# Rounding and splitting streamed weights two row blocks per operation in a hybrid attention and recurrence layer

## The chip, the cores and the metric

The kernel runs on one core of a Trainium2 chip. Its time is the device time of one execution in microseconds (us); the lower, the better. A core has five engines with an instruction stream each: TensorE (PE, matmuls; its weight loads are shown as PEld), VectorE (DVE), ScalarE (ACT), GpSimd (POOL) and SyncE (SP), which here issues most of the DMA transfers. Engines wait for each other by semaphores and otherwise run on their own.

## The reference: what is computed

One layer with 512 tokens of width 2048, in float32. A root-mean-square norm of x is projected by one matrix `w_in` into queries, keys and values, an attention gate, a recurrence input and a recurrence gate. Attention (8 heads, 2 key and value heads, rotary positions) and a gated linear recurrence in both directions run in parallel; each result is normed, multiplied by a gate, and both go through one output matrix `w_out`, with x added.

```
h = rms_norm(x, norm_w)
proj = jnp.einsum('bsd,de->bse', h, w_in)
q, k, v, g_attn, xr, g_lru = jnp.split(proj, SPLITS, axis=-1)
attn_out = attention_group(q, k, v, q_norm_w, k_norm_w)
lru_out = lru_group(xr, conv_w, conv_b, lru_wa, lru_ba, lru_wx, lru_bx, lru_lambda)
mixed = jnp.concatenate([rms_norm(attn_out, attn_norm_w) * jax.nn.silu(g_attn),
                         rms_norm(lru_out, lru_norm_w) * jax.nn.silu(g_lru)], axis=-1)
return x + jnp.einsum('bse,ed->bsd', mixed, w_out)
```

## The kernel before

Every large product is done in three passes of a rounded type (`mm3`, L150 to L154). A float32 operand is split into a high part, rounded to float32r, and a low part, the difference, also rounded. The product is high times high, plus high times low, plus low times high: three matmuls of 128x128 by 128x512 in place of one. Both operands are split. The activations are split once and stay; the weights are streamed and split as they come.

A weight chunk is two row blocks: 256 rows of the matrix by 512 columns. It lands by one DMA in a raw tile `wr` of shape [128, 2, 512] (three such buffers). `wsplit` takes one of the two row blocks: ScalarE copies it to the high tile `wh` (L224, the rounding), then VectorE subtracts high from raw into the low tile `wl` (L226). So a chunk costs two roundings and two subtractions of 512 columns, and fills two high and two low tiles. Each kind of tile has four buffers in the pool `xw`; for a part of the kernel a second pool, `wx`, with four more of each is open, and the halves of a chunk take turns between the two.

The stages, in order of time:

- Two projections of the recurrence input (`proj_feat`, up to about 111 us), with the loading and transposing of x in the first, and the recurrence itself beside the second. Up to the third chunk the order of ScalarE and VectorE is written out by hand; after that the compiler orders them by priority and its estimate of the time. For the very first chunk, the two halves are split at different moments, since its rows land one after the other: the first half is rounded by VectorE in two pieces, the second by ScalarE.
- Keys and values, then queries (`tok_block`, to about 255 us). `wx` is opened during the queries and closed after them.
- The gate stage (`gates`, about 255 to 441 us), beside attention. Two kinds of unit alternate in an order written out as a string: `u`, a chunk of the recurrence gate (`gl_units`: 12 matmuls for two row blocks of 512 columns, some of them with a second operand `dh`, `dl` that is split too, L1199 and L1200), and `G` or `H`, a chunk of a quarter of the attention gate (`ga_units`: two row blocks of 256 columns, split in one operation each, L1227 and L1228, into one narrow tile of each kind). Both kinds draw on the same four buffers in `xw`.
- The rest of the attention gate (`proj_feat`, to about 485 us), while the operands of the output product are split into seven combinations (`seven`, L783 and L784, at 768 and 1024 columns).
- The output product (`outputs`, to the end), with a splitting of its own (`operand`, L802 and L803), its order written out by hand.

TensorE's instructions are issued in the program's order throughout. SyncE issues the weight loads in the order that the compiler gives them; the loads and splits carry a raised priority (`AHEAD = 600`). `paced` (L319) lets GpSimd copy one column of a low tile to hold back transfers of its own until that chunk is split.

Of the kernel before, what the change touches and what calls it, by code (L numbers as in the profile page):

```python
# [12 lines left out]
F32R = mybir.dt.float32r  # L13
# [4 lines left out]
P = 128  # L18
SEQ = 512
# [30 lines left out]
H = 256  # L50
# [12 lines left out]
def hybrid_kernel(  # L63
# [20 lines left out]
    nc = tc.nc  # L84
# [4 lines left out]
    pools, order = {}, {"left": [], "right": []}  # L89
# [25 lines left out]
    def nm(s):  # L115
        cnt[0] += 1
        return f"{s}_{cnt[0]}"
# [27 lines left out]
    def const(shape, name, dt=F32):  # L145
        return cp.tile(list(shape), dt, tag=name, name=name)

    def f(ap):
        return ap.bitcast(F32)
# [34 lines left out]
    def columns(dst, src):  # L184

        n = src.shape[0]
        pt = mm()
        nc.tensor.transpose(pt[:, :n], src, ident[:n, :n])
        with tc.high_priority():
            nc.vector.tensor_copy(dst, pt[:, :n])  # L190
# [22 lines left out]

    turn_of = [0]

    def wsplit(raw, k, rounded=nc.scalar.copy, parts=1):

        turn_of[0] += k
        pool = pools["wx" if "wx" in pools and turn_of[0] % 2 else "xw"]
        hi = pool.tile([P, SEQ], F32R, tag="wh", bufs=4, name=nm("wh"))  # L220
        lo = pool.tile([P, SEQ], F32R, tag="wl", bufs=4, name=nm("wl"))
        cols = [slice(n * SEQ // parts, (n + 1) * SEQ // parts) for n in range(parts)]
        for c in cols:
            rounded(hi[:, c], raw[:, k, c])  # L224
        for c in cols:
            nc.vector.tensor_sub(lo[:, c], raw[:, k, c], f(hi[:, c]))  # L226
        return hi, lo

    def wload(w, r0, c0):
        with tc.high_priority(AHEAD):  # L230
            (raw,) = wraw(w, r0, c0)
            return [wsplit(raw, k) for k in range(2)]


    xh, xl = [None] * KT, [None] * KT
# [824 lines left out]
    with tc.high_priority():  # L1060
        queues = nc.sync, nc.sync
        xs, ws = xload(0, queues), wraw_first(w_in, 0, C_XR, nc.sync)
        nc.scalar.dma_start(nw_st, norm_w.rearrange("(k p) -> k p", p=P))
        xc, raw = next(xs), next(ws)
        next(xs), next(ws)
        table = const([P, 1], "table")
        nc.scalar.activation(table, ones[:, :1], AF.Exp)
        columns(nw, nw_st)
        rest = list(xturn(xc, 0, 2))
        first = [wsplit(raw, 0, nc.vector.tensor_copy, 2)]  # L1070
        for r in rest:
            r()
        busy(WARM2)
# [3 lines left out]
    for step in proj_feat(C_XR, a1, first, given):  # L1077
        if step is None:
            with tc.high_priority():
                first.append(wsplit(raw, 1))  # L1080
                turned_x(xc, 1)
            xsquare(xc, 0)
            next(next(loads), None)
            given[1] = wload(w_in, 2 * P, C_XR)
            continue
        c, e = step
        if (e == 0 or e == 2) and c:
            next(next(loads, iter(())), None)
        if (e, c) == (2, 0) or (e == 1 and c) or (e, c) in ((3, 1), (3, 2)):
            next(next(turns, iter(())), None)  # L1090
        if (c, e) == (1, 2):
            given[2] = wload(w_in, 4 * P, C_XR)
            s2.close()
        if (c, e) == (2, 3):
            vec_load()
        if (c, e) == (5, 3):
            columns(vec, vec_st)
        if c == KT // 2 - 2 and e in (0, 1):
            with tc.high_priority():
                next(stats, None)  # L1100
            gate_maps.setdefault(0, []).extend(itertools.islice(maps, 2))
# [82 lines left out]
    def gl_units(banks):  # L1184

        nd = 0
        for name, left, right in PRODUCTS:
            for c in range(4):
                with tc.high_priority(AHEAD):
                    raw = pools["wr"].tile([P, 2, SEQ], F32, tag="wr", bufs=3, name=nm("wr"))  # L1190
                    nc.sync.dma_start(
                        raw, gsum[c][right] if isinstance(right, int) else two_gl(c, *right)
                    )
                    if isinstance(left, int):
                        draw = draws[nd % 2]
                        nd += 1
                        nc.sync.dma_start(draw, dsum[c][:, left])
                        dh, dl = d_tiles()
                        nc.scalar.copy(dh, draw)  # L1199
                        nc.vector.tensor_sub(dl, draw, f(dh))  # L1200
                    ws = [wsplit(raw, n) for n in range(2)]
                for n, (wh, wl) in enumerate(ws):
                    i = 2 * c + n
                    for s, bank in enumerate(banks):
                        if isinstance(left, int):
                            lh, ll = (t[:, n, s * P : (s + 1) * P] for t in (dh, dl))
                        else:
                            k, t = left
                            ts_ = slice(t * H + s * P, t * H + (s + 1) * P)
                            lh, ll = xh[2 * i + k][:, ts_], xl[2 * i + k][:, ts_]  # L1210
                        mm3(bank, lh, ll, wh, wl, i == 0, i == KT // 2 - 1)
                    if i == KT // 2 - 1:
                        product_done(name, banks)
                    yield name if i == KT // 2 - 1 else None

    def ga_units(part, res, banks):

        for c in range(KT // 2):
            with tc.high_priority(AHEAD):
                raw = pools["wr"].tile([P, 2, SEQ], F32, tag="wr", bufs=3, name=nm("wr"))  # L1220
                src = w_in[c * 2 * P : (c + 1) * 2 * P, C_GA + part * H : C_GA + (part + 1) * H]
                nc.sync.dma_start(raw[:, :, :H], src.rearrange("(k p) e -> p k e", p=P))
                wh, wl = (
                    pools["xw"].tile([P, SEQ], F32R, tag=t, bufs=4, name=nm(t)) for t in ("wh", "wl")
                )
                wh, wl = (t.rearrange("p (k e) -> p k e", k=2) for t in (wh, wl))
                nc.scalar.copy(wh, raw[:, :, :H])  # L1227
                nc.vector.tensor_sub(wl, raw[:, :, :H], f(wh))  # L1228
            for e, bank in enumerate(banks):
                es = slice(e * P, (e + 1) * P)  # L1230
                for k in range(2):
                    kk = 2 * c + k
                    mm3(
                        bank, wh[:, k, es], wl[:, k, es], xh[kk], xl[kk], kk == 0, kk == KT - 1
                    )
                if c == KT // 2 - 1 and e == 1:
                    res.extend(evac_bc(banks))
                yield None
# [165 lines left out]
```

## Time and profile before

| what | value |
|---|---|
| median of 3 runs | 642.55 us (642.46 to 642.91) |
| span of the profiled execution | 640.7 us |
| TensorE busy | 636.0 us, 99% |
| VectorE busy | 509.9 us, 80% |
| ScalarE busy | 382.2 us, 60% |
| GpSimd busy | 131.7 us, 21% |
| roundings of weight blocks at 512 columns (L224, ScalarE) | 151, together 90.1 us |
| subtractions (L226, VectorE) | 153, together 105.6 us |

The profile gives one execution of its own, 640.7 us from its first to its last instruction; the median of the runs is 1.85 us above that span. In the lines below, a row of the timeline gives the start in us from the beginning of the span, the duration in us, the engine, the line of the kernel, the operation, what it writes and reads, its shape, how many in a row, and in square brackets the idle time of the engine before it with what ended it. A row of the groups gives the busy time of the group in us, the mean of one instruction in ns, and the idle time before them. Tile names come without their buffer numbers, and a matmul's row names the moving operand first, then the stationary one.

### The profile page before, as it was taken

The page shows a single profiled execution, that of the slowest core. Times are in us where ns is not written, and L with a number is a line of the kernel's source. Part 1 is how long each engine was busy: PE and PEld are TensorE (multiplying, and loading weights), DVE is VectorE, ACT ScalarE, POOL GpSimd, SP SyncE. Part 2 cuts the span into 40 slices and gives each one's busy share as a digit, 9 for nine tenths or more (in the row PEclk, how much of TensorE's full clock was granted, in tenths as well). Part 3 has the DMA queues.
Part 4 walks back from the last instruction along what each step waited for, and adds up shares of the span by engine and source line. Part 5 has one row for each costly group of instructions (what it writes and reads, how often), then busy time and mean ns, then how long its engine had stood idle before and what let it go on. Part 6 is the DMA issues. An engine that isn't in the chain of part 4 may idle for free.

```text
span 640.7 us, 8950 instructions
## 1 busy us (share of the span) xinstructions
PE 636.0 (99%) x2962; PEld 528.3 (82%) x2962; DVE 509.9 (80%) x886; ACT 382.2 (60%) x725; POOL 131.7 (21%) x173
## 2 busy tenths in 40 slices
PE   9999999999999999999999999999999999999997
PEld 7888888888888888888888888888888888888886
DVE  5777679996698994977678877559938988698994
ACT  3543799489954624877666775946444754344441
POOL 0013403222150501412444353322000000110000
PEclk9999999999999999999999999999999999999999
DMA  8847976897757646445989997875565857585322
GB/s 295 293 140 202 242 203 154 247 252 182 186 158 196 203 135 196 137 141 162 239 241 280 252 253 225 196 209 149 131 196 204 295 175 248 185 281 208 122 93 99
DMA packets 68782, 128.19 MB, mean 200 GB/s; under 512 B 5504, under 2 KB 24320, under 8 KB 68480
## 3 DMA queue, kind: packets, MB, share of 16 engines
q1 hardware_dynamic: 55856, 90.25, 43.2%
q0 software_dynamic: 12704, 37.23, 25.3%
q8 instruction: 23, 0.38, 0.2%
q14 instruction: 23, 0.19, 0.1%
q10 hardware_dynamic: 176, 0.14, 0.1%
HBM read 119.21 MB, written 41.95 MB: 252 GB/s over the span
## 4 chain that ended last, share of the span: by engine, by line
PE 99%; DVE 0%; issue 0%
PE pj L152 19%; PE pj L153 19%; PE pj L154 19%; PE mm L1008 13%; PE pj L1008 11%; PE mm L152 3%; PE mm L154 3%; PE mm L153 3%; PE mm L655 2%; PE mm L256 1%; PE pj L332 1%; PE pj L349 1%; PE mm L591 1%; PE mm L1253 1%; PE mm L1047 0%; PE mm L741 0%
## 5 line engine op out<-in xcount | busy, mean ns | idle before, releaser
L224 ACT CAST wh<-wr 128x512 fp32r<-128x512 f32 x151 | 90.1, 618 | 70.6 <-PE pj L154 25.4
L226 DVE TENSOR_TENSOR wl<-wr,wh 128x512 fp32r<-128x512 f32 (+1 forms) x153 | 105.6, 713 | 30.9 <-ACT wh L224 29.6
L152 PE MATMUL pj<-x,wh 128*128 128x512 f32 x240 | 95.1, 396 | 0.0
L152 PE MATMUL pj<-wh,x 128*128 128x512 f32 x240 | 93.9, 391 | 0.0
L154 PE MATMUL pj<-x,wl 128*128 128x512 f32 x240 | 93.5, 390 | 0.0
L153 PE MATMUL pj<-x,wh 128*128 128x512 f32 x240 | 93.5, 390 | 0.0
L154 PE MATMUL pj<-wh,x 128*128 128x512 f32 x240 | 93.4, 389 | 0.0
L153 PE MATMUL pj<-wl,x 128*128 128x512 f32 x240 | 93.4, 389 | 0.0
L802 ACT CAST oh<-rw 128x512 fp32r<-128x512 f32 x94 | 56.3, 621 | 38.8 <-PE mm L1008 15.5
L803 DVE TENSOR_TENSOR ol<-rw,oh 128x512 fp32r<-128x512 f32 x94 | 61.8, 687 | 10.8 <-ACT oh L802 9.2
L154 PEld LDWEIGHTS pj<-x,wl 128*128 128x128 f32 x240 | 45.0, 188 | 9.7
L154 PEld LDWEIGHTS pj<-wh,x 128*128 128x128 f32 x240 | 45.0, 188 | 9.5
L152 PEld LDWEIGHTS pj<-wh,x 128*128 128x128 f32 x240 | 45.1, 188 | 9.3
L152 PEld LDWEIGHTS pj<-x,wh 128*128 128x128 f32 x240 | 45.1, 188 | 9.2
L153 PEld LDWEIGHTS pj<-wl,x 128*128 128x128 f32 x240 | 45.1, 188 | 9.1
L153 PEld LDWEIGHTS pj<-x,wh 128*128 128x128 f32 x240 | 45.1, 188 | 8.7
L1008 PE MATMUL mm<-oh,ml 128*128 128x512 f32 (+1 forms) x128 | 49.0, 382 | 0.0
L1008 PE MATMUL mm<-ol,mh 128*128 128x512 f32 (+1 forms) x128 | 48.9, 382 | 0.0
L1008 PE MATMUL mm<-oh,mh 128*128 128x512 f32 (+1 forms) x128 | 48.9, 382 | 0.0
L940 POOL DMA_DIRECT2D out_dram<-xt x12 | 6.6, 548 | 178.7 <-DVE xt L976 129.1
L1008 PE MATMUL pj<-oh,mh 128*128 128x512 f32 (+1 forms) x104 | 39.7, 382 | 0.0
L1008 PE MATMUL pj<-ol,mh 128*128 128x512 f32 (+1 forms) x104 | 39.7, 382 | 0.0
(243 smaller groups left out, 1341.4 us busy)
## 6 DMA issues: line engine op xcount, KB each, us to landing
wr<-in_w_in_dram SPq DMA_DIRECT2D x59, 512.0 KB, 4.4
rw<-in_w_out_dram SPq DMA_DIRECT2D x63, 256.0 KB, 3.6
gs<-in_w_in_dram POOLq DMA_DIRECT2D x24, 512.0 KB, 6.8
ts<-in_w_out_dram POOLq DMA_DIRECT2D x24, 512.0 KB, 7.3
wr<-gs SPq DMA_DIRECT2D x16, 512.0 KB, 5.3
rw<-ts SPq DMA_DIRECT2D x31, 256.0 KB, 4.7
wr<-in_w_in_dram SPq DMA_DIRECT2D x17, 256.0 KB, 4.3
gs<-gs POOLq DMA_DIRECT2D x8, 512.0 KB, 7.5
```

Of the source, the lines that this page charges most:

```text
L152: nc.tensor.matmul(acc, lh, rh, start=start, stop=False)
L153: nc.tensor.matmul(acc, lh, rl, start=False, stop=False)
L154: nc.tensor.matmul(acc, ll, rh, start=False, stop=stop)
L224: rounded(hi[:, c], raw[:, k, c])
L226: nc.vector.tensor_sub(lo[:, c], raw[:, k, c], f(hi[:, c]))
L256: nc.tensor.transpose(pt[:, t * P : (t + 1) * P], xc[:, h * n + t, ks], ident)
L332: nc.tensor.matmul(acc[e], w[:, e * P : (e + 1) * P], x_[k], start=k == 0 and j == 0, stop=False,)
L655: nc.tensor.transpose(pt[:, s * P : (s + 1) * P], p[:, s * P : (s + 1) * P], ident)
L802: nc.scalar.copy(hi, src)
L803: nc.vector.tensor_sub(lo, src, f(hi))
L940: (queue or nc.gpsimd).dma_start(of[t * P : (t + 1) * P, os_], xts[g][t][:, cs])
L1008: nc.tensor.matmul(bank[key][:, to], lh[:, a, ts_], rh[:, cols], start=i == 0 and j == 0, stop=i == 7 and j == 2,)
```

## The change

The two row blocks of a chunk are rounded by one ScalarE operation over [128, 2, 512] and subtracted by one VectorE operation of the same shape: 1024 columns in place of 512. The high and low tiles are [128, 2, 512], two buffers of each in place of four narrow ones, so their memory stays the same. `wpair` draws a pair of tiles, and the turn between `xw` and `wx` now goes by pairs. The very first chunk still splits its halves apart, into the two halves of one pair. A unit of the attention gate in the gate stage draws a whole wide pair too and uses 256 of each 512 columns. The matmuls, their order and the transfers are the same.

```diff
--- before.py
+++ after.py
@@ -213,23 +213,26 @@
 
     turn_of = [0]
 
-    def wsplit(raw, k, rounded=nc.scalar.copy, parts=1):
-
-        turn_of[0] += k
+    def wpair():
+
+        turn_of[0] += 1
         pool = pools["wx" if "wx" in pools and turn_of[0] % 2 else "xw"]
-        hi = pool.tile([P, SEQ], F32R, tag="wh", bufs=4, name=nm("wh"))
-        lo = pool.tile([P, SEQ], F32R, tag="wl", bufs=4, name=nm("wl"))
+        return [pool.tile([P, 2, SEQ], F32R, tag=t, bufs=2, name=nm(t)) for t in ("wh", "wl")]
+
+    def wsplit(raw, pair, ks=slice(0, 2), rounded=nc.scalar.copy, parts=1):
+
+        hi, lo = pair
         cols = [slice(n * SEQ // parts, (n + 1) * SEQ // parts) for n in range(parts)]
         for c in cols:
-            rounded(hi[:, c], raw[:, k, c])
+            rounded(hi[:, ks, c], raw[:, ks, c])
         for c in cols:
-            nc.vector.tensor_sub(lo[:, c], raw[:, k, c], f(hi[:, c]))
-        return hi, lo
+            nc.vector.tensor_sub(lo[:, ks, c], raw[:, ks, c], f(hi[:, ks, c]))
+        return [(hi[:, k], lo[:, k]) for k in range(ks.start, ks.stop)]
 
     def wload(w, r0, c0):
         with tc.high_priority(AHEAD):
             (raw,) = wraw(w, r0, c0)
-            return [wsplit(raw, k) for k in range(2)]
+            return wsplit(raw, wpair())
 
 
     xh, xl = [None] * KT, [None] * KT
@@ -1067,7 +1070,8 @@
         nc.scalar.activation(table, ones[:, :1], AF.Exp)
         columns(nw, nw_st)
         rest = list(xturn(xc, 0, 2))
-        first = [wsplit(raw, 0, nc.vector.tensor_copy, 2)]
+        pair = wpair()
+        first = wsplit(raw, pair, slice(0, 1), nc.vector.tensor_copy, 2)
         for r in rest:
             r()
         busy(WARM2)
@@ -1077,7 +1081,7 @@
     for step in proj_feat(C_XR, a1, first, given):
         if step is None:
             with tc.high_priority():
-                first.append(wsplit(raw, 1))
+                first.extend(wsplit(raw, pair, slice(1, 2)))
                 turned_x(xc, 1)
             xsquare(xc, 0)
             next(next(loads), None)
@@ -1198,7 +1202,7 @@
                         dh, dl = d_tiles()
                         nc.scalar.copy(dh, draw)
                         nc.vector.tensor_sub(dl, draw, f(dh))
-                    ws = [wsplit(raw, n) for n in range(2)]
+                    ws = wsplit(raw, wpair())
                 for n, (wh, wl) in enumerate(ws):
                     i = 2 * c + n
                     for s, bank in enumerate(banks):
@@ -1220,10 +1224,7 @@
                 raw = pools["wr"].tile([P, 2, SEQ], F32, tag="wr", bufs=3, name=nm("wr"))
                 src = w_in[c * 2 * P : (c + 1) * 2 * P, C_GA + part * H : C_GA + (part + 1) * H]
                 nc.sync.dma_start(raw[:, :, :H], src.rearrange("(k p) e -> p k e", p=P))
-                wh, wl = (
-                    pools["xw"].tile([P, SEQ], F32R, tag=t, bufs=4, name=nm(t)) for t in ("wh", "wl")
-                )
-                wh, wl = (t.rearrange("p (k e) -> p k e", k=2) for t in (wh, wl))
+                wh, wl = (t[:, :, :H] for t in wpair())
                 nc.scalar.copy(wh, raw[:, :, :H])
                 nc.vector.tensor_sub(wl, raw[:, :, :H], f(wh))
             for e, bank in enumerate(banks):
```

## The prediction

> **What bounds the kernel now.** I read the page's busy shares first, then its chain that ended last, then the waits of TensorE alone, then windows by stage, then single instructions at the places where the change could reach TensorE.
>
> ```profile
> PE 636.0 (99%) x2962; PEld 528.3 (82%) x2962; DVE 509.9 (80%) x886; ACT 382.2 (60%) x725; POOL 131.7 (21%) x173
> ...
> PE 99%; DVE 0%; issue 0%
> ```
>
> ```profile
> PE mm L1047 <- DVE ones L159: 1.0, 1, 1.0
> ```
>
> ```profile
> 0.00:20.00 20.00, 18.93 (x94) 15.05 (x95) 12.03 (x41) 8.24 (x14) 0.76 (x7) 1.00 0.80 264
> 20.00:57.00 37.00, 37.00 (x184) 30.81 (x182) 28.64 (x97) 14.58 (x26) 4.73 (x8) 1.00 0.67 214
> 255.00:441.00 186.00, 186.00 (x920) 155.47 (x919) 141.67 (x242) 135.79 (x291) 66.00 (x81) 1.00 0.76 205
> 485.00:641.00 156.00, 152.10 (x694) 126.57 (x692) 130.21 (x204) 71.03 (x119) 6.57 (x12) 1.00 0.57 196
> ```
>
> The chain is TensorE for 99% of the span. Its one listed wait is 1.0 us before its first matmul; the windows (columns: PE, PEld, DVE, ACT, POOL, then clock, DMA share, GB/s) show it busy without a gap from 20 us on, until the last stores, at the full clock (1.00). A busy row alone proves little, since matmul ends are modelled, so I went to the starts: the 128x512 matmuls quoted below follow each other every 0.227 us in every stage, although one is shown as 0.39 us long. So TensorE is fed without a hole. What ScalarE and VectorE save returns nothing to the span; what they deliver late is added to it in full, because behind any hole TensorE runs on at its one rate.
>
> **What one operation costs.** A pair (two row blocks) is now rounded on ScalarE (L224) and subtracted on VectorE (L226) in two operations each.
>
> ```profile
> L224 ACT CAST wh<-wr 128x512 fp32r<-128x512 f32 x151 | 90.1, 618 | 70.6 <-PE pj L154 25.4
> L226 DVE TENSOR_TENSOR wl<-wr,wh 128x512 fp32r<-128x512 f32 (+1 forms) x153 | 105.6, 713 | 30.9 <-ACT wh L224 29.6
> ```
>
> ```profile
> L784 DVE TENSOR_TENSOR ml<-t,mh 128x1024 fp32r<-128x1024 f32 x8 | 9.8, 1220 | 0.3 <-ACT mh L783 0.3
> L783 ACT CAST mh<-t 128x1024 fp32r<-128x1024 f32 x8 | 8.4, 1053 | 5.8 <-DVE t L774 5.8
> ```
>
> ```profile
> 17.47 1.14 ACT L224 CAST wh<-wr 128x512 fp32r<-128x512 f32 x2
> ...
> 17.04 1.41 DVE L259 SCALAR_TENSOR_TENSOR x<-mm,nw,x 128x512 fp32r<-128x512 f32 x2 [2.12 <-ACT x L258]
> ...
> 19.40 0.42 DVE L269 SCALAR_TENSOR_TENSOR b<-b 128x256 f32<-128x256 f32 x1
> ...
> 19.74 1.29 DVE L226 TENSOR_TENSOR wl<-wr,wh 128x512 fp32r<-128x512 f32 x2
> ```
>
> L783 and L784 do the same two operations at 1024 columns elsewhere: 1.05 and 1.22 us. By the means one would expect a pair to fall from 2 x 618 = 1.24 to 1.05 us, and from 2 x 0.71 = 1.43 to 1.22. But two in a row overlap: they take 1.14 and 1.29. Where they stand in a row, then, the real saving is 0.09 us per pair on ScalarE and 0.07 on VectorE. Over the kernel (151 roundings are 75 pairs and the second half of the first pair, which stays apart) L224 falls from 90.1 to 75 x 1.05 + 0.62 = 79 us busy and L226 from 105.6 to about 75 x 1.22 + 1.4 = 93, none of it on the path. The opposite cost is delivery: the first half's high part comes 1.05 - 0.62 = 0.43 us later, its low part 1.22 - 0.69 = 0.53 us later. Only places with less spare than that matter.
>
> **Place 1: the third chunk of the first projection (20 us).** Here ScalarE and VectorE still run in the written order, and VectorE comes to the subtraction late.
>
> ```profile
> 20.09 0.48 PE L152 MATMUL pj<-x,wh 128*128 128x512 f32 x1
> 20.48 0.19 PEld L154 LDWEIGHTS pj<-x,wl 128*128 128x128 f32 x1
> ```
>
> The low half is done at 19.74 + 0.69 = 20.43 and its weight load starts at 20.48: 0.05 us to spare. One wide subtraction ends at 19.74 + 1.22 = 20.96, so the load waits about 0.5 us. VectorE cannot come earlier: the squares of x (L269) stand ahead of it in the written order, behind L259, which waits for ScalarE at 17.04. Bounds: 0 (if the squares fell behind the subtraction, which the written order excludes) to 0.53. I take **+0.5**.
>
> **Place 2: the last chunk of the second projection (106 us).**
>
> ```profile
> 100.32 0.39 PE L152 MATMUL pj<-x,wh 128*128 128x512 f32 x1
> 105.11 1.29 DVE L226 TENSOR_TENSOR wl<-wr,wh 128x512 fp32r<-128x512 f32 x2
> 105.76 0.39 PE L152 MATMUL pj<-x,wh 128*128 128x512 f32 x1
> 105.99 0.19 PEld L154 LDWEIGHTS pj<-x,wl 128*128 128x128 f32 x1
> ```
>
> A wide subtraction ends at 105.11 + 1.22 = 106.33; the load is due at 105.99: 0.34 us late. TensorE's own 0.5 us of lateness from place 1 lends some of it back, if VectorE's work before is not itself held by TensorE, and the compiler may order VectorE otherwise. Bounds 0 and 0.34; I take **+0.2**, the middle.
>
> In the other chunks of these projections a tile comes free every 24 matmuls, 105.76 - 100.32 = 5.4 us, and rounding and subtracting want 1.05 + 1.22 = 2.27: nothing there. While the second weight pool is open there are four wide pairs instead of eight narrow ones: the same depth.
>
> **Place 3: the gate stage (255 to 441 us).** Units of 12 matmuls alternate between the two gates, and the tiles are one ring. Before, four narrow tiles; a gate unit of 256 columns (L1227, L1228) took one and a recurrence unit two, and the first half came free halfway through its unit. Now there are two wide ones, and either kind takes one, so unit n can be rounded only once unit n-2 is wholly done. The cover is one unit and what attention puts beside it. One of the narrowest:
>
> ```profile
> 335.46 0.39 PE L154 MATMUL pj<-wh,dl 128*128 128x512 f32 x1
> 335.69 0.39 PE L152 MATMUL pj<-wh,dh 128*128 128x512 f32 x1
> 339.20 0.48 PE L152 MATMUL pj<-wh,dh 128*128 128x512 f32 x1
> 339.52 0.40 PE L153 MATMUL pj<-wl,dh 128*128 128x512 f32 x1
> 337.04 0.78 ACT L646 ACTIVATE k<-mm,mx,q_r 128x512 f32<-128x512 f32 x1
> 337.72 0.19 ACT L646 ACTIVATION_READ_ACCUMULATOR k<-mm,mx,q_r 128x1 f32 x1
> 338.44 1.13 DVE L1228 TENSOR_TENSOR wl<-wr,wh 128x512 fp32r<-128x512 f32 x1 [0.28 <-ACT wh L1227]
> ```
>
> The tile is free at 335.69 and its low part is due at 339.52: 3.83 us for 2.27, 1.56 to spare. An exponential with its read (0.97) caught on ScalarE and a subtraction (0.68) on VectorE would use it up and 0.1 more; when VectorE runs stretched (1.13 for a 512-wide one) 0.5 more. I count five such windows (258, 280, 299, 336 and 354 us): 0 to 2.5 us; **+0.1**, since the loads carry the highest priority in that stage. At the stage's end the cover is smallest:
>
> ```profile
> 437.69 0.39 PE L154 MATMUL pj<-x,wl 128*128 128x512 f32 x1
> 440.64 0.39 PE L152 MATMUL pj<-x,wh 128*128 128x512 f32 x1
> 441.10 0.39 PE L154 MATMUL pj<-x,wl 128*128 128x512 f32 x1
> 437.31 1.21 DVE L784 TENSOR_TENSOR ml<-t,mh 128x1024 fp32r<-128x1024 f32 x1
> ```
>
> Free at about 437.92, low part due by 440.9: 3.0 for 2.27. A 1.05 us rounding and a 1.21 us subtraction of the output operands may stand in front: 0 to 1.5; I take **+0.1**.
>
> **Edits at nothing.** The loads on SyncE keep their order and their three buffers; a raw buffer comes free after its second subtraction, as before. GpSimd's marker (L319) waits for the end of the pair as before. The output stage (from 485 us) has its own rounding (L802) and is untouched.
>
> A rule against the change: the Trainium skill, Perfetto Trace Analysis, section Optimizing Scalar/DVE Operations, says grouping pays on a saturated engine, and that where the two are not saturated but hold up another, breaking operations up lets work finish sooner. By its second half the sum holds place 1 and 2 alone, 643.3; by its first half nothing is won with VectorE at 80%, which the trace bears out.
>
> **Sum.** 0.5 + 0.2 + 0.1 + 0.1 = +0.9 us on the profiled span of 640.7, so 641.6. The runs' median, 642.55, stands 1.85 above that span; I keep this: **643.5 us**. Worst of the bounds: 0.53 + 0.34 + 2.5 + 1.5 = 4.9, 647.4.
>
> **Rivals.**
> A, slower: in the gate stage ScalarE, in order, stands at a rounding whose tile is not free, and holds the exponentials behind it; their PSUM banks come late.
>
> ```profile
> 348.78 0.78 ACT L646 ACTIVATE k<-mm,mx,q_r 128x512 f32<-128x512 f32 x1
> 350.11 0.48 PE L152 MATMUL mm<-kt,b 128*128 128x512 f32 x1
> ```
>
> This score bank is read until 349.56 and I take it that the one written at 350.11 is the same: 0.55 us of spare. A hold of 1 us in each of eight heads costs 8 x 0.45 = 3.6 us: 647.1 with the rest. For it: half the depth. Against: the same wait exists already (25.4 us of L224's idle time) and costs nothing. It decides from holds over 0.55 us.
>
> B, slower: the two halves of the first pair now share a tile; were the whole tile waited for, its low part (first loaded at 7.37) would wait for the second half (8.23 + 0.69 = 8.92): +1.5, so 645.0.
>
> ```profile
> 7.37 0.77 PEld L332 LDWEIGHTS pj<-x,wl 128*128 128x128 f32 x4
> 8.23 0.69 DVE L226 TENSOR_TENSOR wl<-wr,wh 128x512 fp32r<-128x512 f32 x1 [0.96 <-ACT wh L224]
> 608.09 0.68 DVE L978 TENSOR_TENSOR xt<-xt,pj 128x512 f32<-128x512 f32 x1
> 608.58 0.54 POOL L940 DMA_DIRECT2D out_dram<-xt  x1 [44.87 <-DVE xt L976]
> ```
>
> Against: at 608 us one half of a tile is written while the store of its other half, ahead of it in the program, has not begun; parts are followed singly.
>
> C, faster: the saved 11 and 13 us bring TensorE work forward. All that could come forward is its first idle 1.07 us (20.00 - 18.93), 641.5, and that lies ahead of any weight.
>
> D, no change: place 1 is absorbed by a shift of VectorE: 642.6.
>
> **How the numbers follow.** Forecast 0.48, A or a large place 3 0.27, B 0.05, C 0.03, D 0.17. A difference under 0.2% (1.3 us) is about what a measurement of this kernel cannot tell from none. The forecast's +0.9 lies inside it, but a fifth of that case reaches over 643.84. Same: 0.17 + 0.38 = 0.55, slower 0.27 + 0.05 + 0.10 = 0.42, faster 0.03. The range runs from D less the scatter of the runs, 642.3, to 646.9, which leaves out C and the upper half of A. The likeliest case's own range is 642.8 to 644.3.
>
> **What would show it.** ScalarE about 371 us and VectorE about 497 busy in all (11 and 13 less); a wide rounding of 1.05 and a wide subtraction of 1.22; a hole of 0.5 us in TensorE's starts near 20.5 us and a smaller one near 106; 0.227 us elsewhere. Many holes between 260 and 441 us would show A. The prediction is wrong if the compiler's new order starves a stage that now has 2 us to spare, or if place 1 does not open.

## The result, and the profile after

The changed kernel took 648.94 us (median of four runs, 648.42 to 650.37), the kernel before 642.66 in the same series: a ratio of 1.0102, 95% interval 1.0088 to 1.0117. The forecast was 643.5 with a range up to 646.9. The profiled execution has a span of 646.3 us and took 648.42. Two executions of a later series, one of the kernel before (918 us at a mean granted clock of 0.66) and one of `one_pair` (1079 us at 0.56), are left out of every ratio below.

The page of the changed kernel: busy shares, the shares of the chain that ended last, and the groups of the rounding and the subtraction (its lines are numbered three higher than before).

```profile
PE 637.1 (99%) x2962; PEld 527.3 (82%) x2962; DVE 501.9 (78%) x811; ACT 373.9 (58%) x650; POOL 133.2 (21%) x173
...
PE 83%; DVE 7%; DMA 4%; ACT 4%; issue 2%; SPq 0%; DVEq 0%; ACTq 0%
...
L227 ACT CAST wh<-wr 128x1024 fp32r<-128x1024 f32 (+1 forms) x76 | 79.0, 1042 | 67.4 <-PE pj L153 22.4
L229 DVE TENSOR_TENSOR wl<-wr,wh 128x1024 fp32r<-128x1024 f32 (+2 forms) x78 | 93.2, 1196 | 31.3 <-ACT wh L227 28.9
```

The groups cost what was forecast, 79 and 93 us. VectorE and ScalarE are each 8 us less busy in all (13 and 11 were forecast; other operations took a little longer). TensorE's share still reads 99%, which tells nothing. The chain tells more: TensorE held 99% of it before and 83% now; VectorE, ScalarE and DMA have come into it. So do TensorE's waits (us in total, times, longest):

```profile
PE mm L152 <- ACT b L487: 2.5, 1, 2.5
PE pj L154 <- DVE wl L229: 1.3, 3, 0.8
PE mm L1050 <- DVE ones L159: 1.0, 1, 1.0
PE pj L152 <- ACT ev L555: 0.3, 1, 0.3
```

Before, only the third of these (as L1047) was there. Since TensorE's matmuls come in the same order in both, I subtracted the start of each matmul before from its start after; every jump of that difference is a hole. In this trace: 0.5 us at 20 us (place 1), **2.7 at 95 us**, 1.1 at 106 (place 2), 0.7 at 209 (queries), 0.35 from 350 to 358, 0.55 at 441 (end of the gate stage, at 446 here); the first loads gave some 0.5 back. At its end TensorE is 5.4 us late.

**The hole of 2.7 us** is in the second projection, where the recurrence's gate products (`mm<-k,k`) run between the weights. The timeline of the changed kernel, rows of five engines followed backward from the hole:

```profile
98.17 0.50 PE L152 MATMUL mm<-k,k 128*128 128x512 f32 x1 [2.49 <-ACT b L487]
...
92.07 0.69 ACT L487 ACTIVATE b<-mm,vec 128x512 f32<-128x512 f32 x1
95.97 0.62 ACT L460 CAST k<-k 128x512 fp32r<-128x512 f32 x1 [3.21 <-DMA k<-in_lru_wx_dram]
...
82.66 0.37 SPq L203 DMA_DIRECT2D wr<-in_w_in_dram  x1
83.08 0.46 SPq L538 DMA_DIRECT2D k<-in_k_norm_w_dram  x1
...
92.93 0.38 SPq L441 DMA_DIRECT2D k<-in_lru_wa_dram  x1
...
91.15 0.23 DVE L541 COPY k<-k 128x128 f32<-128x128 f32 x1 [3.62 <-DMA k<-in_k_norm_w_dram]
...
91.48 1.43 DVE L546 TENSOR_TENSOR rk<-rk,k 128x256 f32<-128x256 f32 x4
...
81.37 1.07 POOL L857 DMA_DIRECT2D gs<-in_w_in_dram  x1 [5.16 <-issue]
```

TensorE waits for a bank of PSUM (the memory that matmuls write) that ScalarE's sigmoids (L487) have to read. ScalarE has done one sigmoid at 92.07 and then stands at the rounding of the next gate map (L460), whose second load lands only at 95.9. SyncE issued the map's two loads at 92.93 and 93.36, right behind the end of VectorE's L546 at 92.91; I read this as a buffer that VectorE gives back late. VectorE was late because it had stood 3.62 us at the copy of the key norm's weights (L541). Before, the same steps were:

```profile
78.00 1.07 POOL L854 DMA_DIRECT2D gs<-in_w_in_dram  x1 [2.80 <-issue]
...
82.49 0.46 SPq L535 DMA_DIRECT2D k<-in_k_norm_w_dram  x1
...
87.54 0.23 DVE L538 COPY k<-k 128x128 f32<-128x128 f32 x1
...
89.27 1.90 SPq L438 DMA_DIRECT2D k<-in_lru_wa_dram  x4
...
94.66 1.85 ACT L484 ACTIVATE b<-mm,vec 128x512 f32<-128x512 f32 x3
...
96.39 0.64 ACT L457 CAST k<-k 128x512 fp32r<-128x512 f32 x1
```

The key-norm load lands 5.0 us after its issue before and 8.0 us after. What differs at that moment is GpSimd's pair of 512 KB transfers (L857, L860): 78.0 and 78.6 us before, 81.4 and 82.0 now, 1.7 us ahead of SyncE's key-norm load. In both traces GpSimd issues the first transfer of each pair 0.3 to 0.4 us after the first one of the pair ahead has landed, so a delay at the front of this chain travels. It also grows: the first transfer of the chain is 1.26 us later than before (53.69 against 52.43, of which the marker's longer copy is 0.85), this one 3.4. Most of the growth is in two landings on the way, 7.65 and 7.38 us after their issue in place of 6.46 and 6.69; why they took longer is not shown. The front, GpSimd and VectorE, of the changed kernel:

```profile
52.47 1.22 DVE L229 TENSOR_TENSOR wl<-wr,wh 128x1024 fp32r<-128x1024 f32 x1
...
52.63 1.11 POOL L322 COPY mark<-wl 128x1 f32<-128x1 f32 x1
```

and of the kernel before:

```profile
51.74 0.69 DVE L226 TENSOR_TENSOR wl<-wr,wh 128x512 fp32r<-128x512 f32 x1
...
52.22 0.26 POOL L319 COPY mark<-wl 128x1 f32<-128x1 f32 x1
```

A copy of one column, GpSimd's first marker, takes 1.11 us in place of 0.26: it ends 0.04 us behind the subtraction that it ran into. That subtraction belongs to the ninth pair (the first chunk of the second projection), another chunk than the one the marker reads, so this is no wait for data. My theory: this collision starts the chain of transfers late, and the chain's later pair then comes out just ahead of the norm loads. The rivals: the order on ScalarE (the rounding L460 stood behind the fourth sigmoid before and stands behind the first now), or simply the later delivery of all wide operations.

### The profile page after: what moved, and what is told of

It reads as the page before. It is cut to its first block, busy times and chain, and to the rows that moved or that the text cites. A ratio compares the mean times of both kernels' runs of the same rounds, so it can differ in the third digit from the quotient of the medians.

```text
span 646.3 us, 8722 instructions
## 1 busy us (share of the span) xinstructions
PE 637.1 (99%) x2962; PEld 527.3 (82%) x2962; DVE 501.9 (78%) x811; ACT 373.9 (58%) x650; POOL 133.2 (21%) x173
## 4 chain that ended last, share of the span: by engine, by line
PE 83%; DVE 7%; DMA 4%; ACT 4%; issue 2%; SPq 0%; DVEq 0%; ACTq 0%
PE pj L154 15%; PE pj L152 15%; PE pj L153 15%; PE mm L1011 13%; PE pj L1011 11%; PE mm L152 3%; DMA wr<-in_w_in_dram 3%; PE mm L153 3%; PE mm L154 3%; PE mm L658 2%; DVE wl L229 2%; DMA k<-in_k_norm_w_dram 1%; PE pj L335 1%; PE mm L259 1%; ACT wh L227 1%
## 5 line engine op out<-in xcount | busy, mean ns | idle before, releaser
L227 ACT CAST wh<-wr 128x1024 fp32r<-128x1024 f32 (+1 forms) x76 | 79.0, 1042 | 67.4 <-PE pj L153 22.4
L229 DVE TENSOR_TENSOR wl<-wr,wh 128x1024 fp32r<-128x1024 f32 (+2 forms) x78 | 93.2, 1196 | 31.3 <-ACT wh L227 28.9
```

The lines of the kernel that those rows point to most:

```text
L227: rounded(hi[:, ks, c], raw[:, ks, c])
L229: nc.vector.tensor_sub(lo[:, ks, c], raw[:, ks, c], f(hi[:, ks, c]))
```

## The experiments

A jump of TensorE's lateness is called a hole below; "at 95" and so on names its place. Where an expectation numbers the theories, theory 1 is the order on ScalarE and theory 3 the chain that begins at the marker; another is spelled out in its text.

**The order on ScalarE.** `hold_maps`: the changed kernel, with the gate map's rounding tied behind the fourth sigmoid as before (`sig` collects the sigmoids).

```diff
...
-                nc.scalar.copy(gh, gr)
+                with tc.issue_after(sig[-5]) if len(sig) == 16 else ExitStack():
+                    nc.scalar.copy(gh, gr)
...
```

> The changed kernel, with one edge added: ScalarE's rounding of the first gate map of the second recurrence half (L460) is queued behind the fourth sigmoid, where the kernel before has it, in place of behind the first. Theory 1 (the compiler's new order on ScalarE let that rounding stand in front of sigmoids while its load was late, and TensorE ran out of PSUM banks): the hole of 2.65 us near 95 us closes, later ones move with it: 648.9 - 2.7 = 646.2, and less if VectorE's lateness near 106 us shrinks too. Theory 2 (wide operations as such make the recurrence late): the hole stays, 648.5 to 649.

650.96 us, ratio 1.0121 (1.0087 to 1.0155). The hole at 95 is gone, and the loss came back 11 us later: VectorE still stood 3.23 us for the key-norm load, and the last chunk's low part was late.

```profile
PE pj L154 <- DVE wl L229: 3.6, 3, 3.1
```

So, with the key-norm load late (7.7 us to its landing here), the order decides where the loss shows, not whether. The reverse, `maps_first_before`: the kernel before with the loads of the first gate map put first on SyncE, by which the rounding takes the place it has after (`both` collects the second load of each map).

```diff
-            with tc.high_priority(AHEAD):
+            with tc.high_priority(AHEAD), tc.issue_after(both[0]) if half and both else ExitStack():
...
```

> The kernel before, with the loads of that first gate map put ahead of the other three maps' loads on SyncE; the compiler then orders its rounding on ScalarE right behind the first sigmoid, as in the changed kernel. Theory 1a (the order alone costs it): a hole of about 2 us near 95 us, 644.5. Theory 1b (order and a late load are both needed): here the load lands near 92 us and ScalarE comes to the rounding near 94.7, so no hole: 642.6.

643.35 us, ratio 1.0011 (1.0000 to 1.0022), with a hole of 0.6 us at 95. Order alone is worth a fifth of the hole.

**Tiles or operations.** Three kernels keep the changed kernel's wide tiles and do a pair by two narrow operations where a condition on the pair's number holds: always in `tiles_only`; for pairs 9 to 16, the second projection, in `xr2_narrow` (the diff shown); for all others in `xr2_wide_only`.

```diff
+        if ks == slice(0, 2) and (9 <= turn_of[0] <= 16):
+            for k in range(2):
+                nc.scalar.copy(hi[:, k], raw[:, k])
+                nc.vector.tensor_sub(lo[:, k], raw[:, k], f(hi[:, k]))
+            return [(hi[:, k], lo[:, k]) for k in range(2)]
```

> The changed kernel's wide tiles, two buffers of each, but every pair rounded and subtracted by two operations of 512 columns as before. The compiler's order of ScalarE in the recurrence is that of the changed kernel. Theory 1 (half of the loss is the order that the tiles brought, the rest late delivery by wide operations): the holes of 0.5 us near 20 us and near 445 us close, the one near 95 us stays if its load is late again: 645 to 646. Theory 2 (all of it is the width of the operations): 642.6.

> The changed kernel with the eight pairs of the second projection alone (50 to 106 us) rounded and subtracted by two operations of 512 columns. Theory 3: GpSimd's transfers go out early again, no hole near 95 and under 0.5 near 106; the holes near 20 and 445 us (0.5 each), and a small one near 209 and 350, stay: 644 to 644.5. If the loss is spread over all wide operations: about 647.

> The opposite: wide operations in the second projection alone, two of 512 columns everywhere else, on the wide tiles. Theory 3: the holes near 95 and 106 us are there, 3.7 together, the others not: 646.5 to 647. If the loss is spread: 644.

`tiles_only` took 643.53 us, ratio 1.0010 (1.0001 to 1.0020), with one hole, 0.65 at 106. ScalarE's order is that of the changed kernel here too: it is the tiles that change the compiler's order, not the operations. `xr2_narrow` took 645.87 (1.0031 to 1.0064): no hole at 95, the marker at 0.60 us, and holes of 0.5 at 20, 0.8 at 106, 1.0 at 209 and 0.55 at 441; its median lies above the 644 to 644.5 expected, and its ten executions scatter from 644.5 to 648.3. `xr2_wide_only` took 643.94 (1.0003 to 1.0026) with holes of 1.2 at 106 and 0.5 at 408, none at 20, 95 or 441; the expected large hole failed to appear, and so did its cause, for the marker began at 52.35, ahead of the subtraction at 52.97, and took 0.24 us. Place 1 and the stage's end follow the width of their own operations in every one of these runs.

**The marker and the transfers.** `no_mark` leaves the first marker copy out of the changed kernel; `slots` moves GpSimd's pair near 80 us to a later stage; `one_pair` does the ninth pair alone (`turn_of[0] == 9` in the condition above) by narrow operations. `no_mark_2` and `one_pair_2` are the same kernels again, beside an unedited one; `one_pair` itself has times, but no trace that can be compared.

```diff
-            nc.gpsimd.tensor_copy(mark[:, 0:1], f(ws[1][1][:, 0:1]))
+            if c0 != C_XR:
+                nc.gpsimd.tensor_copy(mark[:, 0:1], f(ws[1][1][:, 0:1]))
```

```diff
-SLOTS = {C_XR: (7,), C_XR + SEQ: (0, 1, 2, 3, 6, 7), C_K: range(8), C_Q: (3, 4)}
+SLOTS = {C_XR: (7,), C_XR + SEQ: (0, 1, 2, 6, 7), C_K: range(8), C_Q: (3, 4, 5)}
```

> The changed kernel, with GpSimd's transfers tied to the fourth chunk of the second projection (two of 512 KB, which went out at 81 us together with SyncE's loads at 82 to 83 us) left to later chunks; the order on ScalarE stays that of the changed kernel. Theory 1c (the gate maps were late because the load before them, of the key norm, took 8.0 us in place of 5.0 beside those transfers): it lands in 5 us again, the maps 3 us earlier, the hole of 2.65 us closes to under 0.5 and the one of 1.0 near 108 us to under 0.5: 645.5. If the transfers have nothing to do with it: 648.9.

> The changed kernel without GpSimd's first marker, the one that took 1.11 us beside a wide subtraction (0.26 in the kernel before); GpSimd's transfers start about 1 us earlier. Theory 3a (that stretched marker starts the lateness of GpSimd's transfers): the pair that went out at 81.4 goes out at 79 to 80, the holes near 95 and 106 us shrink from 3.7 together to 1 or 2: 646.5. If the lateness comes from elsewhere: 648.9.

> The changed kernel with one single pair (the ninth, the first chunk of the second projection) rounded and subtracted in two narrow operations each; every other pair stays wide. Theory (one wide subtraction beside GpSimd's first marker copy starts the large loss): the marker takes at most 0.6 us, GpSimd's pair of transfers goes out by 79 to 80 us, the key-norm load lands in 4 to 6 us, the hole near 95 us (2.7) is gone, those at 20 us (0.5), near 106 us (0.7 to 1.1) and at 445 us (0.5) stay: 645.8 to 646.7. Rival (the wide operations of the whole second projection cost it, the marker does not matter): the hole near 95 us stays, 648.4 to 650.4.

> The changed kernel with the ninth pair alone in narrow operations, again, beside the unedited one. Theory: the marker ends at most 0.7 us after it began, the hole near 95 us is gone, holes of 0.5 at 20 and 445 us and about 0.7 to 1.1 near 106 us stay: 644.4 to 646.2, at or below the median of the unedited kernel and without its executions over 647. Rival: the same spread as the unedited kernel and a hole near 95 us.

> The changed kernel without GpSimd's first marker copy, again, beside the unedited one. Theory: no hole near 95 us, and 644.4 to 646.7, at or below the unedited kernel's median. Rival (the marker does not matter): the same times as the unedited kernel, with executions over 647.

| kernel | time, us | ratio to before | hole at 95 | GpSimd's pair at | marker, us |
|---|---|---|---|---|---|
| `slots` | 646.04 (645.53 to 648.18) | 1.0049 (1.0032 to 1.0066) | none | moved | 1.02 |
| `no_mark` | 646.72 (645.55 to 647.25) | 1.0054 (1.0035 to 1.0072) | none | 78.7 | left out |
| `one_pair` | 645.26 (644.15 to 648.18) | 1.0041 (1.0024 to 1.0059) | no trace | | |
| `one_pair_2` | 645.78 (644.22 to 649.15) | 1.0056 (1.0038 to 1.0074) | none | 78.65 | 0.73 |
| `no_mark_2` | 646.10 (644.73 to 647.63) | 1.0056 (1.0044 to 1.0068) | none | 79.1 | left out |
| unedited (`after_third`), beside the last two | 648.50 (648.18 to 650.20) | 1.0101 (1.0086 to 1.0115) | 2.55 | 82.9 | 1.09 |

Each way of sparing the chain takes the hole away. In `slots` the marker is caught as well, and without the pair among the norm loads no hole opens at 95. One narrow pair of 75 is enough, for 2.7 us. But the gain is not 5.4, and with the hole gone others of 0.4 to 1.8 us sometimes stood at 204, 209 and 350 us (in `slots` and `no_mark_2`), so these kernels scatter too. Leaving the marker out also has a price of its own, a hole of 0.35 (`no_mark`) and 0.7 us (`no_mark_2`) at 57 us.

Can it be made with narrow operations? `gs_late` and `gs_collide` are the kernel before with GpSimd's pair near 80 us tied to the fifth chunk in place of the fourth. In `gs_late` it is tied to the low part (the first edit below alone), in `gs_collide` to the high one, which is ready earlier (both edits).

```diff
-SLOTS = {C_XR: (7,), C_XR + SEQ: (0, 1, 2, 3, 6, 7), C_K: range(8), C_Q: (3, 4)}
+SLOTS = {C_XR: (7,), C_XR + SEQ: (0, 1, 2, 4, 6, 7), C_K: range(8), C_Q: (3, 4)}
...
-            nc.gpsimd.tensor_copy(mark[:, 0:1], f(ws[1][1][:, 0:1]))
+            nc.gpsimd.tensor_copy(mark[:, 0:1], f(ws[1][0 if (c0, c) == (C_XR + SEQ, 4) else 1][:, 0:1]))
```

> The kernel before, narrow throughout, with GpSimd's two transfers of about 78 us tied to the next weight chunk, so that they go out at about 82 us, together with SyncE's loads of 82 to 83 us, as in the changed kernel. Theory 3 (the collision of those transfers is what costs, whatever the width of the operations): the key norm's load lands near 91 us in place of 87.5, VectorE stands at it, and a hole of 2 to 3 us opens in TensorE near 106 us (near 95 only a little, since ScalarE's order here has three sigmoids ahead of the gate map): 645 to 646. Theory 2 (wide operations as such): 642.6.

> The kernel before, narrow operations and tiles, with one edit: GpSimd's pair of transfers near 80 us is tied to the high tile of the fifth chunk of the second projection in place of the low tile of the fourth, so it goes out about 3 us later, some 1 us ahead of SyncE's key-norm load. Theory (it matters that the pair goes out just ahead of the key-norm load): that load takes 7 to 8 us in place of 5.0, VectorE stands at the transposed copy behind it, and a hole of 1 to 3 us opens near 95 to 106 us: 643.7 to 645.7. Rival (the transfers' order does not matter with narrow operations): 642.5 to 643.0 and no hole.

`gs_late` took 642.99 (ratio 0.9989 to 1.0013): the pair went out at 82.36, 0.2 us behind the key-norm load (82.16), which still landed in 5.0 us; the pair itself took 9 to 10, and the query-norm load 7.3 in place of 3.3, without a hole at 95 or 106. `gs_collide` took 644.10, ratio 1.0019 (1.0009 to 1.0029). Rows of its timeline, and the answer on the key-norm load:

```profile
81.04 1.07 POOL L854 DMA_DIRECT2D gs<-in_w_in_dram  x1 [0.39 <-issue]
...
82.26 0.47 SPq L535 DMA_DIRECT2D k<-in_k_norm_w_dram  x1
...
90.57 0.23 DVE L538 COPY k<-k 128x128 f32<-128x128 f32 x1 [3.35 <-DMA k<-in_k_norm_w_dram]
...
107.21 0.50 PE L154 MATMUL pj<-x,wl 128*128 128x512 f32 x1 [1.08 <-DVE wl L226]
...
DMA to landing us min/median/max: 8.3/8.3/8.3
```

With nothing wide in the kernel, the pair 1.2 us ahead of the load brings back the 8 us landing and VectorE's stand of 3.35 us. Between these two kernels, which of the two is issued first decides how long the key-norm load takes. With the order of before on ScalarE the loss shows at 106, 1.4 us, and 1.2 more in smaller holes from 350 to 412 us. The late pair together with the new order on ScalarE was not tried in a narrow kernel, so the hole at 95 itself has been taken away, but not made, by an edit.

**All places at once.** `four_pairs`: pairs 3, 9, 16 and 85 narrow, those at the places of 20, 95, 106 and 441 us.

> The changed kernel with four of its pairs in narrow operations: the 3rd (20 us), the 9th and the 16th (first and last chunk of the second projection) and the 85th (late in the stage of the attention gate). Theory (four places carry the loss, the other seventy-odd pairs cost nothing): holes at 20, 95 and 445 us are gone, the one near 106 us shrinks to the 0.6 that the wide tiles' order alone showed: 643.4 to 644.6. Rival (later delivery costs a little in many stages): 645.5 or more with new holes between 200 and 445 us.

644.03 us (643.03 to 646.67), ratio 1.0023 (1.0011 to 1.0035). All four holes are gone or under 0.2 us; one of 0.65 at 209 stays, and TensorE ends 0.37 us behind before. The first loads came 0.6 us early in this execution; counted from 19 us on, it is 1.0 behind. So some seventy wide pairs cost TensorE about 1 us together, and four cost most of the rest. No version came out below the kernel before, and none could by much: TensorE had 1.07 us to give.

**The unedited kernel again.** Five more traces of it.

> The changed kernel once more, unedited, to see what of its holes returns. Theory: the holes at 20 us (0.5), 95 us (about 2.7), 106 us (about 1) and 445 us (0.5) return, since each hangs on a fixed order or on a collision that the schedule repeats; those at 209 and 350 us (0.6 and 0.25) may not: 648.4 to 650.4. Rival (the collision at 52 us is a matter of chance): some of the runs at 646 and a profile without the hole near 95 us.

> The changed kernel, unedited, for a third trace. Theory (the hole near 95 us opens in those executions in which GpSimd's first marker copy begins while VectorE subtracts the ninth pair): if the trace shows the marker at 1 us or more, it shows the hole (2.5 to 3 us) and 647 to 650; if the marker takes 0.3 us or less, there is no hole near 95 us and the time is 644.2 to 645.8 (place 1 with 0.5, the last chunk of the second projection with 0.6 to 1.1 and the end of the gate stage with 0.5 alone). Times of both kinds in the series. Rival (the hole has another cause): marker and hole do not go together.

> The changed kernel, unedited, one execution for a fourth trace. The same as for after_third: marker at 1 us or more together with a hole of 2.5 to 3 us near 95 us and 647 to 650, or marker at 0.3 us or less together with no such hole and 644.2 to 645.8.

> The changed kernel, unedited, a fifth trace. Theory: marker at 1 us or more together with a hole of 1.9 to 3 us near 95 us and 647 to 650, or marker at 0.3 us or less together with no such hole and 644.2 to 645.8. Rival: a time under 646 with the marker caught, or over 647 with it free.

> The changed kernel, unedited, a sixth trace. Theory: marker at 1 us or more together with a hole of 1.9 to 3 us near 95 us, 647 to 649 at full clock and up to 650.4 where the granted clock drops behind the hole; or marker at 0.3 us or less together with no such hole and 644.2 to 645.8. Rival: a time under 646 with the marker caught, or over 647 with it free.

| trace | time, us | marker, us | 20 | 95 | clock behind it | 106 | 209 to 212 | 441 |
|---|---|---|---|---|---|---|---|---|
| first | 648.42 | 1.11 | 0.5 | 2.7 | | 1.1 | 0.7 | 0.55 |
| `after_again` | 647.32 | 1.29 | 0.5 | 3.0 | | 0.4 | 0 | 0.55 |
| `after_third` | 648.28 | 1.09 | 0.5 | 2.55 | 1.7 | 0 | 0.45 | 0.6 |
| `after_fourth` | 647.72 | 1.19 | 0.5 | 2.0 | | 1.4 | 0.1 | 0.55 |
| `after_fifth` | 648.74 | 1.20 | 0.55 | 2.55 | 1.7 | 0 | 0 | 0.6 |
| `after_sixth` | 645.54 | 0.24 | 0.5 | 0 | | 0.5 | 0.8 | 0.6 |

In the sixth the marker slipped through, 0.2 us ahead of the subtraction, and the chain behind it runs about as it did before (rows of its timeline):

```profile
53.01 0.24 POOL L322 COPY mark<-wl 128x1 f32<-128x1 f32 x1
...
53.21 1.22 DVE L229 TENSOR_TENSOR wl<-wr,wh 128x1024 fp32r<-128x1024 f32 x1
...
78.39 1.07 POOL L857 DMA_DIRECT2D gs<-in_w_in_dram  x1 [2.62 <-issue]
...
88.41 0.23 DVE L541 COPY k<-k 128x128 f32<-128x128 f32 x1 [0.21 <-DMA k<-in_k_norm_w_dram]
...
93.33 0.61 ACT L460 CAST k<-k 128x512 fp32r<-128x512 f32 x1
```

ScalarE's order is still the new one here (L460 behind one sigmoid), and costs nothing, since the load is in time. This is the same program: in these traces it is decided by 0.2 us between GpSimd, which waits for a small transfer of its own, and VectorE. Where the marker is caught, the norm load that VectorE stands at is the key's (first trace), the query's (`after_again`), or both in turn. In `after_again` GpSimd's pair went out at 84.60, behind both norm loads; the key's landed in 4.0 us, and yet the query's was late:

```profile
90.41 0.23 DVE L540 TENSOR_SCALAR k<-k 128x128 f32<-128x128 f32 x1 [2.88 <-DMA k<-in_q_norm_w_dram]
```

In the other three the pair went out 0.2 to 0.3 us ahead of the key-norm load, which landed in 5.5 to 5.8. So in the unedited kernel, whose two norm loads follow each other closely, the loss goes with the pair near them, and not with one order of issue. In all five the gate maps' loads begin at 92.0 to 93.6 us, in the sixth at 90.3. Of 19 executions of the changed kernel in all, 12 took 647.3 to 650.4 and 7 took 644.3 to 645.8, none between. Only six have a trace; that the others divide by the same cause is likely, not shown. The series differ (6 of 8 low in the one of `after_again`, whose median of 645.39 has a ratio of 1.0041, 1.0027 to 1.0055; 0 of 4 in two others); why is open. The series of `after_again` and of `after_third` ran on different chips, and whether that matters was not tried.

Some of these executions have a second part: the mean granted clock is 0.994 to 0.997 in those of 648.28, 648.74, 648.77, 649.12 and 650.37 us, and 0.999 or more in the others (650.20 among them, which stays open). `after_third`, windows behind the hole (columns as in the prediction: PE, PEld, DVE, ACT, POOL, clock, DMA share, GB/s) and TensorE's rows:

```profile
90.00:97.00 7.00, 5.67 (x25) 4.35 (x24) 5.43 (x11) 3.84 (x5) 0.00 (x0) 1.00 0.73 240
...
98.00:100.00 2.00, 1.93 (x5) 1.54 (x6) 2.00 (x3) 2.00 (x5) 0.16 (x1) 0.51 0.24 72
100.00:102.00 2.00, 2.00 (x7) 1.61 (x6) 2.00 (x3) 1.41 (x3) 2.00 (x3) 0.64 0.56 115
...
106.00:120.00 14.00, 14.00 (x64) 11.59 (x63) 12.50 (x17) 10.47 (x12) 2.67 (x6) 1.00 0.73 211
```

```profile
98.07 0.79 PE L152 MATMUL mm<-k,k 128*128 128x512 f32 x1 [2.41 <-ACT b L487]
98.67 0.63 PE L153 MATMUL mm<-k,k 128*128 128x512 f32 x1
99.09 0.63 PE L154 MATMUL mm<-k,k 128*128 128x512 f32 x1
```

Behind the hole the granted clock falls, to a mean of 0.51 in the first of these windows, and matmuls follow each other every 0.42 us in place of 0.227, until about 101.4. That costs 1.7 us more here and 1.7 in `after_fifth`. By the mean clock of the two windows the low rate lasted 2 x 0.49 / 0.5 + 2 x 0.36 / 0.5 = 3.4 us, and the windows of `after_fifth` (0.92, 0.50, 0.73) give 3.4 as well.

## Why the prediction was wrong

By its own steps:

- **The price of the operations: right.** 1.05 and 1.22 us, 79 and 93 us in all, and nothing of what was saved came back.
- **Place 1, +0.5: right.** 0.5 to 0.55 in all six traces, and gone wherever pair 3 was narrow. The subtraction starts at 19.30, the weight load stands for its end:

```profile
19.30 1.22 DVE L229 TENSOR_TENSOR wl<-wr,wh 128x1024 fp32r<-128x1024 f32 x1
...
20.57 0.19 PEld L154 LDWEIGHTS pj<-x,wl 128*128 128x128 f32 x1 [0.66 <-DVE wl L229]
```

- **Place 2, +0.2 of 0 to 0.34: mis-sized.** The mechanism was right, but 0.4 to 1.4 us opened (1.1 in the profiled execution) in four traces of six; in the two without, TensorE was already 4.2 and 5.0 us late behind the hole and the clock. `tiles_only` shows 0.65 from the new order alone. I had let a change of order only lessen this term; my upper end took VectorE's order as given.
- **Place 3, the stage's end, +0.1 of 0 to 1.5: mis-sized, in bounds.** 0.55 to 0.6 in all six traces. Two operations do stand in front, but both are VectorE's, a subtraction of the output operands at 768 columns and an evacuation; the rounding that I had feared was done before:

```profile
443.64 0.94 DVE L787 TENSOR_TENSOR ml<-hs,mh 128x768 fp32r<-128x768 f32 x1
444.51 0.68 DVE L430 TENSOR_TENSOR ev<-pj,rbc 128x512 f32<-128x512 f32 x1
445.11 1.21 DVE L229 TENSOR_TENSOR wl<-wr,wh 128x1024 fp32r<-128x1024 f32 x1
```

- **Place 3, the windows within the stage, +0.1:** 0 to 0.35 in the six traces. Right.
- **Edits at nothing: this is the step that failed.** Two of its sentences were wrong. "The loads on SyncE keep their order": the query-norm load went from 87.3 to 83.6 us, right behind the key's (83.1), and the gate maps' loads changed places among themselves. And "GpSimd's marker (L319) waits for the end of the pair as before": I priced the marker by the data that it waits for, not by the engine beside which it runs. The second was the dear one: the marker took 1.1 to 1.3 us in five of six traces, and with it went the hole at 95 us, 2.0 to 3.0 us, and 1.7 more in two of them by the clock. So "behind any hole TensorE runs on at its one rate" did not hold in these two either.
- **Rival A had the mechanism in the wrong stage.** ScalarE, in order, stood at a rounding and held what was behind it until PSUM ran out: with sigmoids at 95 us, not exponentials in the gate stage. Its own hole, at 350 us, was at most 0.35 in the unedited kernel; 0.4 to 1.8 in three of the others.
- **Rivals B, C and D** fell: no trace shows the first pair's low half waiting for the second half, nothing came forward, and place 1 opened.
- **What the sum lacked besides:** 0 to 0.8 us at 209 us, where ScalarE's evacuation (L555) comes behind work held by VectorE; and 0.35 us around the span, which is 2.1 to 2.2 us in the changed kernel and 1.7 to 1.8 in the one before. The cause of the latter is open: `four_pairs` has it and `one_pair` does not.

With the terms as measured, all holes but that at 95 us come to 1.2 to 3.1 us in the six traces. With the 0.35 around the span that is 1.6 to 3.5, or 644.1 to 646.0 us, where the seven low executions lie (644.3 to 645.8). The hole and the clock add 2.0 to 4.3, up to 650.3, which is about where the twelve high ones end (647.3 to 650.4).

One reading was off without changing a term: an exponential with its read takes 0.87 us by the rows shown (337.04 to 337.91), not 0.97, so with the subtraction it would just have used up the 1.56 of spare.

The sentence of the Trainium skill, Perfetto Trace Analysis, section Optimizing Scalar/DVE Operations, that the prediction weighed came out on its second half: the engines that saved were not the limit, and breaking up the operations of four pairs again brought what TensorE lost behind 19 us from 2.25 us (`after_sixth`, with the marker free) to 1.0 (`four_pairs`).

## What to carry to other kernels

Where one engine is fed without a hole, price a wider operation by the work that runs beside it and the order that follows it, not by its own saving: look up every instruction of the neighbour engines that starts during it, above all the small ones that begin a chain of transfers. A compiler that orders by estimates may reorder other engines for a changed tile shape, as ScalarE's and SyncE's order here; separate tile from operation by one kernel each before explaining anything. And a difference of starts, matmul by matmul, between two traces with the same order finds all holes at once, where busy shares showed none.

## What the runs showed of the hardware

- **GpSimd's copy stands still beside VectorE's subtraction.** Free, the one-column copy took 0.20 to 0.24 us. Begun between 0.04 us ahead of the wide subtraction's start and 0.17 us behind it, it took 1.09 to 1.29 and ended 0.02 to 0.04 us behind the subtraction's end in all five traces; beside a narrow one (`one_pair_2`) it took 0.73. The 0.26 of before was of that kind too: it ended 0.04 us behind the narrow subtraction that it met near its end. The Trainium skill, SBUF — State Buffer, section SBUF: two separate sides, says that VectorE and GpSimd share one pair of ports, held for a whole instruction by whichever starts first, and that a VectorE operation with two SBUF inputs takes it against a GpSimd operation that reads SBUF. These traces agree, but for one thing that they cannot show: in `after_again` the copy that was held up began 0.04 us ahead of the subtraction by the profile's starts, so these do not tell which of the two took the ports first.
- **A small load among large transfers of another queue landed up to 5 us later.** The key-norm load took 5.0 us with GpSimd's pair of 512 KB transfers begun 4.5 us ahead of it or 0.2 us behind, 5.5 to 5.8 with the pair begun 0.2 to 0.3 us ahead, 7.7 to 8.3 with it begun 1.2 to 1.8 us ahead, and 3.4 with no pair near (`slots`). What of the transfers collides is not shown.
- **TensorE's clock can halve behind an idle stretch of 2.4 us.** After two such stretches, both of 2.4 us, the granted clock was 0.5 for 3.4 us; after others of 1.8 to 3.1 us it stayed at 1.0. The Trainium skill, TensorE: Matmul & The Clock Gate, section What's actually happening, gives these two rates and a free-running window of about 3.4 us. Such a window fits the length, and a phase that is free would fit that the fall comes after some of these stretches and not after others. But the Trainium skill puts the slow state after at least one idle window of that length, and that was not needed here, since no idle stretch was so long.
